# Fewer w_ada sums among the scan's matrix builds, more behind them, and attention at the splits' priority

## The chip, the cores and the metric

The kernel runs on one core of one Trainium2 chip. The metric is the device time of one execution in microseconds. The core's engines are TensorE (PE: matmuls, and PEld: its weight loads), VectorE (DVE), ScalarE (ACT), GpSimd (POOL) and SyncE (SP, which here issues DMAs only). The profiler records one execution; its times are counted from the first instruction.

## The reference

A decoder block on one sequence of 256 positions and width 2048, all in float32:

```python
mod = silu(c) @ w_ada + b_ada                        # 2048 x 12288: six vectors of 2048
sh1, sc1, g1, sh2, sc2, g2 = split(mod, 6)
h = rms_norm(x, norm_mix_g) * (1 + sc1) + sh1
u, q, k, v, ga, gb = split(h @ w_in)                 # 2048 x 8192
y_ssm = s5_branch(u, ...)                            # a complex diagonal scan over the sequence, gelu, GLU
y_att = moba_attention(q, k, v, rel_bias)            # 8 heads of 128; one block of 256, so plain causal softmax
merged = sigmoid(ga) * (y_ssm @ w_proj_ssm) + sigmoid(gb) * (y_att @ w_proj_attn)
x = x + g1 * (merged @ w_out)
h2 = rms_norm(x, norm_mlp_g) * (1 + sc2) + sh2
x = x + g2 * (square(relu(h2 @ w_ff1)) @ w_ff2)      # 2048 x 8192 and back
return rms_norm(x, norm_final_g)
```

## The kernel before

**Weights.** All large weights are streamed from HBM in tiles of 128 x 1024 floats (512 KB): 128 tiles of `w_in`, 16 of each projection, 8 of the GLU, 32 of `w_out`, 256 of the MLP. `stream` does this for a list of tiles: SP issues the load into one of seven `wraw` buffers; `split` (L175, L177) makes a rounded high part `whi` on ACT and the remainder `wlo` on DVE, in four buffers each; then PE multiplies high by high, high by low and low by high, into four PSUM banks. `gemm_n` (L313 to L317, banks `pn`), `gemm_t` (L257 to L259, `pt`) and `gemm_d` (L276, L280, `pd`) differ in which operand stands still. So a tile asks DVE and ACT for one operation each, and the DMA engines for one load.

**The order of the work.** The program text emits instructions; a planner (`schedule_with_timeline_sim=True`) then orders each engine's instructions by an estimate of when their operands are ready, and among those that are ready by priority. Priority is the order of emission, a lower number first. `high_priority(offset=n)` sets an instruction n places ahead; the weights' loads and splits in `stream` run under `OFF = 300`. `issue_after` puts an instruction behind a named one on its engine. On the chip each engine then takes its instructions in the order written.

**Lanes.** Work beside the streams is kept in lanes, lists of small jobs. After each weight tile `step` adds a lane's rate to its credit and runs as many jobs as the credit has whole units. So a rate of 0.5 means a job for every second weight tile. Four lanes matter here:

- "ada": the sums of `w_ada` with silu(c). Up to `hjob(14)` these are 24 wide ones (L419), from which the 16 slices of h come. Behind them stand 96 narrow jobs and one more (the list `late`): each issues a 512 KB load into a `wraw` buffer (L370) and multiplies the one loaded before by the spread vector on DVE, with a running sum (L377). They make sc2, sh2 and g1; the first 16 serve the first quarter of h2. 32 later ones make g2 beside the MLP. The rate is set in turn to R1, R2 (at `hjob(8)`), R3 (at `hjob(14)`), R4 (when lane "ssm" is flushed), RS0, RSM and RS2 (for the three gate gemms), RS3 and others behind.
- "ssm" (`ssm_builds`): the bias vector, then the scan's matrices. `ssm_build1` in four parts and `ssm_build3` in two are complex products on DVE (`cmul`, L713 to L715, 36 instructions in jobs of two) with scratch `tt` in slot "T"; `ssm_build1` fills `bp`, `ssm_build3` fills `cc`. `ssm_build2`, eight jobs, transposes `bp` on PE (L748) and copies it back on ACT (L753).
- "rk" (`ssm_build4`): four blocks of 64 small PE matmuls with `cc` (L783), each evacuated by ACT and DVE (L787, L788); then `ssm_lag`, 16 DMAs on SP of short rows (L797) from slot "S5".
- "m": attention's jobs (`attn_jobs`), then the scan itself. Per head, `attn1` does the scores on PE (L840, L841), adds the bias `tz` on DVE (L843, L844), and the softmax on DVE and ACT; `attn2` transposes on PE (L859); `attn3` multiplies by v (L867, L868) and copies to `yatt` on ACT (L870). `yatt` takes slot "S5" when `ssm_lag` has read it. The PSUM banks of all this, `rk` included, are three, tagged "ax".

**Around the change**, in the order of emission: the last units of u (8 tiles) and k (8 tiles) of `w_in`, beside which the builds run; POOL's 32 DMAs of `hop_in`; the flush of "ssm"; `bias_load`, four POOL DMAs that fill `tz` (slot "T" too, 256 KB each, L587); v's unit (8 tiles) with lane "rk" and from its fourth tile the first attention jobs; three gate gemms of 16 tiles with the rest of attention and the scan (`vr`, `vi` L933, `ys` L971 and L974, `sri` L954 to L959); and then w_proj_attn, the GLU, w_proj_ssm, w_out and the MLP. `make_h` makes h2; its last quarter, just before the first `pd` gemm, needs the last of the `late` sums.

Of the kernel before, what the change touches and what calls it, by code (L numbers as in the profile page):

```python
# [39 lines left out]
OFF = 300  # L40
# [6 lines left out]
SL = 22  # L47
R1 = .75
R2 = .75
R3 = .5  # L50
R4 = .9
RS0 = .4
RSM = .1
RS2 = .35
RS3 = .7
GR = (1, 3, 4, 8)
RAT = 1.4
# [19 lines left out]
class Kern:  # L77
# [721 lines left out]
    def ssm_builds(self):  # L799
        return ([self.bias_prep, self.ssm_load_bc] + [lambda: None] * 3 + [self.bias_write]  # L800
                + sum([self.parts(self.ssm_build1, i) for i in range(4)], []) + [self.ssm_cc]
                + sum([self.parts(self.ssm_build3, i) for i in (0, 1)], [])
                + [lambda i=i, b=b: self.ssm_build2(i, b) for i in range(2) for b in range(4)])

    def pairs(self, kts):
# [66 lines left out]
    def attn_jobs(self):  # L872
        def job(*fs):
            def run():
                for f, h in fs:
                    f(h)
            return run

        jobs = [job((self.attn1, h)) for h in range(3)]
        for h in range(H):  # L880
            jobs.append(job((self.attn2, h)))
            jobs.append(job((self.attn3, h), (self.attn1, h + 3)) if h + 3 < H else job((self.attn3, h)))
        return jobs
# [105 lines left out]
    def body(self):  # L989
# [243 lines left out]
        def hjob(k0):  # L1233
            def f():
# [5 lines left out]
                if k0 == 14:  # L1240
                    self.lanes["ada"][1] = R3
                    self.lanes["ssm"][1] = SR2
# [76 lines left out]
        self.flush("ssm")  # L1319
        self.lanes["ada"][1] = R4  # L1320
        self.bias_load()
# [32 lines left out]
        for i in range(1, 4):  # L1354
            if i > 1:
                self.lanes["ada"][1] = (RSM, RS2)[i - 2]
            dst, c0 = ((ga, 4096), (ga, 5120), (gb, 6144), (gb, 7168))[i]
# [360 lines left out]
```

## Time and profile before

| what | value |
|---|---|
| time, median of 3 runs | 1362.84 us (1361.17 to 1363.31) |
| the profiled execution | 1363.43 us, span 1361.7 us |
| PE busy | 1344.0 us, 99% of the span |
| DVE busy | 1037.9 us, 76% |
| ACT busy | 748.9 us, 55% |
| HBM read | 350.79 MB, 259 GB/s over the span |
| chain that ended last | PE 92%, DVE 3%, ACT 3%, issue 1% |

The times of an engine are the unions of its instructions' times. PE's instructions overlap, so their starts tell more than their durations. A wait is an engine's idle time before an instruction, with what ended it. The median's bounds lie 2.1 us apart.

### The profile page before, as it was taken

The numbers are of one execution on the slowest core, as the hardware profiler recorded it, in microseconds if no ns is written. First come the engines' busy times: TensorE is split into PE (matmuls) and PEld (weight loads), VectorE is DVE, ScalarE is ACT, GpSimd is POOL, SyncE is SP. The second block draws the span as 40 slices with busy tenths as digits, with TensorE's granted clock in tenths as the row PEclk, the third lists the DMA queues.
The fourth block names the chain that finished last, engine by engine and source line by source line (L and its number), as shares of the span: only waits on it lengthen the run. The fifth ranks groups of instructions, "written<-read, shape, count | busy, mean of one in ns | idle before, by whom it ended". The sixth has DMA issues, their size and how long they took to land.

```text
span 1361.7 us, 21535 instructions
## 1 busy us (share of the span) xinstructions
PE 1344.0 (99%) x8278; PEld 1168.1 (86%) x8278; DVE 1037.9 (76%) x1438; ACT 748.9 (55%) x1045; POOL 42.8 (3%) x93
## 2 busy tenths in 40 slices
PE   9999999999999999999999999999999999999997
PEld 8898899788888988888999888888888888888885
DVE  7888998866997888988887967686766555555677
ACT  7767557468448553455555655453554544535543
POOL 0000004000004000000000000000000000000000
PEclk9999999999999999999999999999999999999999
DMA  9999998986378888987797878888878566566552
GB/s 380 407 409 410 377 314 257 285 243 199 105 225 264 292 297 280 337 327 288 269 366 270 285 225 275 228 267 288 246 243 240 192 190 188 190 190 196 181 194 70
DMA packets 116825, 357.09 MB, mean 262 GB/s; under 512 B 16561, under 2 KB 16705, under 8 KB 116305
## 3 DMA queue, kind: packets, MB, share of 16 engines
q1 hardware_dynamic: 113488, 349.61, 75.9%
q0 software_dynamic: 2800, 5.70, 1.4%
q8 instruction: 65, 1.06, 0.3%
q10 hardware_dynamic: 432, 0.40, 0.1%
q14 instruction: 40, 0.32, 0.1%
HBM read 350.79 MB, written 2.51 MB: 259 GB/s over the span
## 4 chain that ended last, share of the span: by engine, by line
PE 92%; DVE 3%; ACT 3%; issue 1%; DMA 0%; ACTq 0%; DVEq 0%
PE pn L313 18%; PE pn L315 18%; PE pn L317 17%; PE pd L276 14%; PE pd L280 7%; PE pt L259 5%; PE pt L257 5%; PE pt L258 5%; ACT whi L175 1%; DVE wlo L177 1%; PE ys L971 1%; PE vr L933 0%; ACT pn L224 0%; PE rk L783 0%; PE sco L841 0%
## 5 line engine op out<-in xcount | busy, mean ns | idle before, releaser
L177 DVE TENSOR_TENSOR wlo<-wraw,whi 128x1024 fp32r<-128x1024 f32 x448 | 545.4, 1222 | 255.9 <-ACT whi L175 253.0
L175 ACT CAST whi<-wraw 128x1024 fp32r<-128x1024 f32 (+1 forms) x449 | 467.4, 1051 | 468.0 <-PE pn L315 204.6
L276 PE MATMUL pd<-h2h,whi 128*128 128x512 f32 x800 | 209.4, 393 | 0.0
L313 PE MATMUL pn<-whi,ff 128*128 128x512 f32 x496 | 193.0, 389 | 0.0
L315 PE MATMUL pn<-whi,ff 128*128 128x512 f32 x496 | 193.0, 389 | 0.0
L317 PE MATMUL pn<-wlo,ff 128*128 128x512 f32 x496 | 191.6, 389 | 0.0
L276 PEld LDWEIGHTS pd<-h2h,whi 128*128 128x128 f32 x800 | 140.2, 189 | 21.4
L377 DVE SCALAR_TENSOR_TENSOR wraw<-wraw,cb 128x1024 f32<-128x1024 f32 x128 | 155.9, 1218 | 0.0
L280 PEld LDWEIGHTS pd<-h2h,wlo 128*128 128x128 f32 x800 | 116.6, 190 | 12.8
L313 PE MATMUL pn<-whi,ah 128*128 128x512 f32 x320 | 125.7, 397 | 1.4 <-ACT pn L224 0.7
L315 PE MATMUL pn<-whi,ah 128*128 128x512 f32 x320 | 126.1, 394 | 0.0
L280 PE MATMUL pd<-h2h,wlo 128*128 128x256 f32 x800 | 119.9, 281 | 0.0
L317 PE MATMUL pn<-wlo,ah 128*128 128x512 f32 x320 | 113.5, 391 | 0.0
L317 PEld LDWEIGHTS pn<-wlo,ff 128*128 128x128 f32 x496 | 93.1, 188 | 19.3
L315 PEld LDWEIGHTS pn<-whi,ff 128*128 128x128 f32 x496 | 93.2, 188 | 19.1
L313 PEld LDWEIGHTS pn<-whi,ff 128*128 128x128 f32 x496 | 93.1, 188 | 19.1
L257 PE MATMUL pt<-ah,whi 128*128 128x256 f32 x384 | 104.5, 284 | 0.2 <-DVE tz L601 0.2
L258 PE MATMUL pt<-ah,whi 128*128 128x256 f32 x384 | 104.1, 283 | 0.0
L259 PE MATMUL pt<-ah,wlo 128*128 128x256 f32 x384 | 92.5, 284 | 0.7 <-DVE wlo L177 0.7
L257 PEld LDWEIGHTS pt<-ah,whi 128*128 128x128 f32 x384 | 73.4, 192 | 1.4 <-ACT whi L175 0.8
L313 PEld LDWEIGHTS pn<-whi,ah 128*128 128x128 f32 x320 | 59.9, 188 | 16.0 <-ACT whi L175 1.5
L258 PEld LDWEIGHTS pt<-ah,whi 128*128 128x128 f32 x384 | 73.4, 192 | 0.2
(379 smaller groups left out, 1995.5 us busy)
## 6 DMA issues: line engine op xcount, KB each, us to landing
wraw<-in_w_ff_dram SPq DMA_DIRECT2D x256, 512.0 KB, 4.9
wraw<-in_w_in_dram SPq DMA_DIRECT2D x128, 512.0 KB, 6.3
wraw<-in_wat_dram SPq DMA_DIRECT2D x128, 512.0 KB, 5.7
ahm<-in_wat_dram SPq DMA_DIRECT2D x48, 512.0 KB, 10.2
wraw<-in_w_out_dram SPq DMA_DIRECT2D x32, 512.0 KB, 6.1
wraw<-in_w_proj_attn_dram SPq DMA_DIRECT2D x16, 512.0 KB, 6.6
wraw<-in_w_proj_ssm_dram SPq DMA_DIRECT2D x16, 512.0 KB, 6.0
ahm<-in_wan_dram SPq DMA_DIRECT2D x8, 512.0 KB, 10.4
```

Source lines behind the costliest of these rows:

```text
L175: h = self.nc.scalar.copy(hi[:, c], src[:, c])
L177: s = self.nc.vector.tensor_sub(lo, src, hi.bitcast(F32))
L257: nc.tensor.matmul(o, hi[:, c], xh[:, kx, :], start=st, stop=False, skip_group_check=True)
L258: nc.tensor.matmul(o, hi[:, c], xl[:, kx, :], start=False, stop=False, skip_group_check=True)
L259: self.mm = nc.tensor.matmul(o, lo[:, c], xh[:, kx, :], start=False, stop=sp, skip_group_check=True)
L276: nc.tensor.matmul(banks[blk], hi[:, cut(blk, k)], x2[:, ks[k], :, :], start=i + k == 0, stop=False, skip_group_check=True)
L280: self.mm = nc.tensor.matmul(banks[blk][:, S:2 * S], lo[:, cut(blk, k)], x2[:, ks[k], 0, :], start=False, stop=last and k == 1, skip_group ...
L313: nc.tensor.matmul(o, xh[:, kx, tk], hi[:, c], start=q == 0 and not full, stop=False, skip_group_check=full)
L315: nc.tensor.matmul(o, xl[:, kx, tk], hi[:, c], start=False, stop=False, skip_group_check=full)
L317: self.mm = last = nc.tensor.matmul(o, xh[:, kx, tk], lo[:, c], start=False, stop=q == n - 1, skip_group_check=full)
L377: v.scalar_tensor_tensor(w, w, 1.0, self.cb[:, (i % 2) * 1024:(i % 2 + 1) * 1024], op0=OP.mult, op1=OP.mult, accum_out=pc[:, i:i + 1])
L971: nc.tensor.matmul(p[q, c], self.cc[q, i, j].rearrange("p s c -> p (s c)"), self.sri[q, b % 2, i, c], start=i == 0, stop=False)
```

## The change

Two edits. First, the rates of the "ada" lane. From `hjob(14)` to the end of the builds on DVE it runs at 0.15 in place of 0.5. A new job in lane "ssm", between `ssm_build3` and `ssm_build2`, sets it to R5 = 0.9; the flush of "ssm" then sets R4, now 0.6 in place of 0.9. Beside the second gate gemm it runs at 0.2 (0.1 before), beside the third at 0.3 (0.35 before). Second, every attention job runs under `high_priority(offset=OFF)`, as the loads and splits of weights do.

```diff
-R3 = .5
-R4 = .9
+R3 = .15
+R4 = .6
+R5 = .9
 RS0 = .4
-RSM = .1
-RS2 = .35
+RSM = .2
+RS2 = .3
...
     def ssm_builds(self):
...
-                + sum([self.parts(self.ssm_build3, i) for i in (0, 1)], [])
+                + sum([self.parts(self.ssm_build3, i) for i in (0, 1)], []) + [lambda: self.pace("ada", R5)]
                 + [lambda i=i, b=b: self.ssm_build2(i, b) for i in range(2) for b in range(4)])
...
     def attn_jobs(self):
         def job(*fs):
             def run():
-                for f, h in fs:
-                    f(h)
+                with self.tc.high_priority(offset=OFF):
+                    for f, h in fs:
+                        f(h)
             return run
```

## Prediction

> **What bounds the kernel now.** I read the page's busy times first, then the waits of PE behind the start-up, then PE's timeline around the longest of them, then the DMA queues and DVE's groups there. The page's head and three of its rows:
>
> ```profile
> span 1361.7 us, 21535 instructions
> PE 1344.0 (99%) x8278; PEld 1168.1 (86%) x8278; DVE 1037.9 (76%) x1438; ACT 748.9 (55%) x1045; POOL 42.8 (3%) x93
> ...
> q8 instruction: 65, 1.06, 0.3%
> ```
>
> PE is the bound. The change adds and removes no instruction: all 128 `w_ada` sums, all splits and all matmuls stay, in another order. So it can only win or lose idle time of PE. From 150 us to 660 us, which holds nearly all that the edit touches, PE's waits are these:
>
> ```profile
> PE rk L783 <- issue: 2.9, 1, 2.9
> PE pn L313 <- ACT pn L224: 0.7, 1, 0.7
> PE ys L971 <- DVE sri L956: 0.5, 1, 0.5
> PE ys L971 <- DVE sri L959: 0.2, 1, 0.2
> ```
>
> That is 4.3 us, of which 2.9 in one place, among the `rk` matmuls of `ssm_build4`. PE's timeline there (start, duration, count; idle time before in brackets):
>
> ```profile
> 266.81 1.02 PE L783 MATMUL rk<-cc,cmp 64*32 64x64 f32 x57
> 270.69 0.44 PE L783 MATMUL rk<-cc,cmp 64*32 64x64 f32 x7 [2.85 <-issue]
> 271.05 0.79 PE L840 MATMUL sco<-qk 128*128 128x128 f32 x2
> ...
> 272.49 0.63 PE L840 MATMUL sco<-qk 128*128 128x128 f32 x2
> ...
> 273.42 0.83 PE L315 MATMUL pn<-whi,ah 128*128 128x512 f32 x1
> 274.08 0.39 PE L317 MATMUL pn<-wlo,ah 128*128 128x512 f32 x1
> 274.31 0.39 PE L313 MATMUL pn<-whi,ah 128*128 128x512 f32 x1
> ...
> 277.28 0.38 PE L840 MATMUL sco<-qk 128*128 128x128 f32 x2
> ...
> 277.75 0.58 PE L315 MATMUL pn<-whi,ah 128*128 128x512 f32 x1
> ```
>
> The pause costs more than 2.85 us, since the work behind it runs slowly. From the last `rk` before it (266.81 + 1.02 = 267.83) to the first gemm matmul at the usual pace (274.08) are 6.25 us. At full pace that work takes 1.30 us: two heads' scores at 277.75 - 277.28 = 0.47 each, seven `rk` at 1.02 / 57 each, 0.13, and one gemm matmul, 274.31 - 274.08 = 0.23. **The place costs 4.95, say 5.0 us.** The granted clock says why (window, then length, PE, PEld, DVE, ACT, POOL busy, PEclk, DMA share, GB/s):
>
> ```profile
> 236.00:258.00 22.00, 21.34 (x115) 16.86 (x114) 22.00 (x28) 11.86 (x15) 0.43 (x1) 1.00 0.87 291
> 258.00:271.00 13.00, 10.15 (x260) 8.18 (x258) 7.58 (x13) 4.74 (x10) 1.52 (x4) 0.98 1.01 252
> 271.00:290.00 19.00, 19.00 (x88) 15.82 (x83) 13.13 (x25) 11.96 (x26) 0.00 (x0) 0.92 0.77 195
> 339.00:360.00 21.00, 20.25 (x334) 17.14 (x333) 20.30 (x28) 8.23 (x12) 0.27 (x2) 1.00 0.33 100
> ```
>
> The same rows show what else is full: DVE, 22.00 of 22.00 us before the pause, and the DMA engines, 1.01 in it. "issue" means that the profile shows no semaphore that PE waits for. I read it as late instructions: 2 x 8278 PE instructions came in 65 fetches, 255 each. The DMA view of 254.6 to 267.7 us, and then of 267.7 to 269.1 us:
>
> ```profile
> q1 hardware_dynamic: 685, 2.50, 64.9%
> q0 software_dynamic: 166, 0.97, 34.6%
> ```
>
> ```profile
> q8 instruction: 1, 0.02, 5.6%
> ```
>
> ```profile
> 253.80:261.04 7.24, 7.24 (x131) 1.00 0.97 314
> 261.04:267.83 6.79, 6.79 (x155) 1.00 1.02 211
> ```
>
> Thirteen microseconds without a fetch, while PE ran 286 matmuls with as many weight loads, 2.2 fetches' worth. Then one fetch, and PE goes on. What fills the DMAs is weights and sums (q1) and POOL's bias table `tz` (q0). By the view of its line:
>
> ```profile
> L587 POOL DMA_DIRECT2D tz<-scr x4: 489/494/497, 257.6 to 259.0; - x4
> L587 POOLq EVENT_SEMAPHORE  x1: 25267/25267/25267, 231.8 to 231.8; - x1
> ...
>   DVE cc L715: 25.3, 1
> ...
> DMA to landing us min/median/max: 7.1/10.0/12.0
> ```
>
> POOL was free at 231.8 and stood 25.3 us for `cc`, the last of the scan's matrices on DVE: `tz` takes their scratch. The `rk` matmuls wait for the same `cc`. So the late builds bring table and burst together.
>
> **The change part by part.** A lane takes one step per weight tile. From `hjob(14)` to the last `ssm_build3` part are 14 steps: 14 x 0.5 = 7 jobs of the "ada" lane before, 14 x 0.15 = 2 after. To the flush are 10 more: 5 before, 9 after at 0.9. Then, before and after: v's unit (8 steps) 7 and 4; three gate gemms (16 each) 6, 2, 5 and 7, 3, 5. From there the rates are the old ones, and the lane is two jobs behind until it ends. DVE's groups from 160 to 258 us:
>
> ```profile
> L177 DVE TENSOR_TENSOR wlo<-wraw,whi 128x1024 fp32r<-128x1024 f32 x33 | 40.1, 1220 | 7.6 <-ACT whi L175 7.6
> L377 DVE SCALAR_TENSOR_TENSOR wraw<-wraw,cb 128x1024 f32<-128x1024 f32 x18 | 21.9, 1217 | 0.0
> ```
>
> Eighteen sums ran before `cc` was done; those 21.9 us stood between builds and splits. With two to eight left, the last build ends 10 to 16 sums earlier, 12 to 19 us, near 238 to 245 instead of 257. (The "ada" sums have a split's loads too: five fewer jobs before the last build, three fewer in v's unit, 512 KB each.) `tz` is issued as much earlier and lands after 7.1 to 12.0 us; the four `rk` blocks then come a tile apart instead of crowded, with less on q1 beside them. No row shows that arrangement, so its price has two ends: the whole 5.0 us gone, or the pause whole. I take it as gone, nearest the row of 339 to 360 us, where 334 matmuls, many as small, ran at a DMA share of 0.33 without "issue". The waits for L224 (0.7) and `sri` (0.7) I cost at nothing; gone, they are the end 1.4 us lower.
>
> [...]
>
> **Attention's priority.** The offset lifts its operations level with the splits, by program order. Work per head is unchanged; PE stays the bound while it waits for none. Now its score additions (L843, L844) can stand on DVE ahead of later splits, and they wait for `tz`; its `yatt` copies stand on ACT ahead of later casts and wait for `ssm_lag`'s landing, as `yatt` takes that slot. Behind both are splits, and PE waits for those. I cost it at nothing while whi and wlo's four buffers cover it; without cover, see the second rival. A row that bounds the cover: DVE's splits around the pause,
>
> ```profile
> 265.51 1.23 DVE L177 TENSOR_TENSOR wlo<-wraw,whi 128x1024 fp32r<-128x1024 f32 x1 [2.30 <-ACT whi L175]
> ...
> 272.74 0.38 DVE L843 SCALAR_TENSOR_TENSOR asc<-sco,tz 128x128 f32<-128x128 f32 x1 [0.98 <-PE sco L841]
> ...
> 275.78 1.20 DVE L177 TENSOR_TENSOR wlo<-wraw,whi 128x1024 fp32r<-128x1024 f32 x1
> ```
>
> none for 9 us, in which PE did some 2.5 us of gemm (273.42 to 275.78) without a wait. So the cover is 2.5 us at least, and at most four tiles of 12 matmuls at 0.23, 11 us.
>
> **SP's queue.** `ssm_lag` is emitted where it was, and holds SP:
>
> ```profile
> 271.82 13.78 SPq L797 DMA_DIRECT2D rt<-cmp  x16
> 285.71 0.54 SPq L370 DMA_DIRECT2D wraw<-in_wat_dram  x1
> ```
>
> The weights' loads are behind it, as before. PE waited for nothing there, so again nothing; it moves up with `rk`.
>
> **The two late jobs.** The sums end two tiles later before the last `make_h`. Its last split and the `pd` gemm that uses it:
>
> ```profile
> 724.95 0.69 DVE L177 TENSOR_TENSOR h2h<-htmp,h2h 128x512 fp32r<-128x512 f32 x1 [1.18 <-ACT h2h L175]
> ```
>
> ```profile
> 724.27 0.63 PE L276 MATMUL pd<-h2h,whi 128*128 128x512 f32 x2
> ...
> 735.43 2.00 PE L276 MATMUL pd<-h2h,whi 128*128 128x512 f32 x8
> ...
> 738.22 2.00 PE L276 MATMUL pd<-h2h,whi 128*128 128x512 f32 x8
> ```
>
> A `pd` step is 738.22 - 735.43 = 2.79 us; that split is needed in the fourth, near 732.7, and is done at 725.6. Two tiles of 24 matmuls at about 0.12 (half of 0.23) shift it by 5.6 us: hidden, with 1.5 us to spare.
>
> **The sum.** The profiled execution took 1363.43 us (span 1361.7, 1.7 around it), 0.6 over the median of the three runs, 1362.84. 1363.4 - 5.0 = **1358.4 us**, -0.33% of the median. With the other 1.4 us also gone, 1357.0.
>
> **Rivals.**
>
> *The pause stays or moves.* The builds pull `tz` and `rk` forward together, and a block of `rk` is 64 pairs, 128 instructions a tile; with the tile's own 24 a fetch lasts under two tiles, some 6 us, and `tz` alone lands over 7.1 to 12.0 us. Or the burst itself starves PE, whatever the DMAs do. For it: the 0.87 share before the pause, to which the table is added. Against: 334 matmuls in 21 us without one. Time 1361 to 1365, centre 1363.4. [...]
>
> *Slower: attention blocks DVE before its table has landed.* The planner that orders each engine puts the first score addition on DVE where it expects `tz`. If the table lands by its median 10.0 us where the plan has it at once, DVE stands 10.0 us with splits behind it; over a cover of 2.5 us PE idles 7.5, and loses another 2.1 to the clock (5.0 - 2.9 above). 1358.4 + 9.6 = 1368.0. It decides from a lateness of the cover, 2.5 to 11 us, plus the 5.0 won. For it: attention ran behind everything before, and the first L843 waited for PE alone, `tz` being there. Against: fewer sums leave DVE more lead than the trace of before shows.
>
> **How the numbers follow.** Forecast 0.48 (own range 1356.5 to 1360), pause stays or moves 0.30, slower 0.22. A measurement of this kernel tells about 0.2%, 2.7 us, from no change: faster is under 1360.1, slower over 1365.6. The forecast lies below the first; of the second case I give 0.02 to faster. So faster 0.50, same 0.28, slower 0.22. The range, 1356 to 1367, leaves out a little below the floor of 1357.0 and the larger half of the slower case.
>
> **What would show it.** Right: no "issue" wait of PE at `rk`, PEclk 1.00 from 236 to 290 us; `tz` issued before 246; at most eight L377 before the last `cc`; PE's sum of waits from 150 to 660 us near 1.4 us. Wrong: L783 again waiting for issue; or DVE idle before L843 until `tz`, or ACT before L870, followed by PE waiting for `whi` or `wlo`. If the pause goes and the time stays, the reading of its price is wrong.

## The result

The changed kernel takes 1371.2 us (median, 1370.3 to 1374.0) against 1363.0 us (1361.2 to 1363.3) for the kernel before in the same comparison: a ratio of 1.0067, 95% interval 1.0049 to 1.0084. It is slower by 0.67%. The forecast was 1358.4 us, and the time lies above the whole range. The profiled execution took 1371.07 us with a span of 1369.3 us, 7.6 us longer than the span of before.

Lines of the kernel file are one higher than before, and two higher behind `attn_jobs`: L783 is now L784, L313 to L317 are L314 to L318, L224 is L225, L377 is L378, L715 is L716, L587 is L588.

The head of the page of the changed kernel: as many PE instructions as before, with the same work.

```profile
span 1369.3 us, 21532 instructions
PE 1346.4 (98%) x8278; PEld 1167.9 (85%) x8278; DVE 1037.8 (76%) x1438; ACT 751.0 (55%) x1045; POOL 42.9 (3%) x93
```

PE's waits in the changed kernel from 150 to 1360 us (total, times, longest):

```profile
PE pn L314 <- issue: 4.4, 1, 4.4
PE pn L314 <- ACT pn L225: 2.8, 2, 2.3
PE pn L318 <- DVE wlo L178: 0.5, 1, 0.5
PE pn L314 <- ACT whi L176: 0.5, 1, 0.5
PE pt L258 <- ACT whi L176: 0.4, 1, 0.4
PE pt L260 <- DVE wlo L178: 0.2, 1, 0.2
```

Two changed most. The pause with no releaser is back, 4.4 us where it was 2.9. The wait for ACT's copy into `pn` grew from 0.7 to 2.8. The scan's `sri` waits, 0.7 together, are gone. Four small waits for splits are new, 1.6 us together. All of them add up to 8.8 us, where near 1.4 was forecast.

The table of attention did come earlier. Its line in the changed kernel:

```profile
L588 POOL DMA_DIRECT2D tz<-scr x4: 492/494/497, 244.2 to 245.7; - x4
...
  DVE cc L716: 10.2, 1
...
DMA to landing us min/median/max: 6.9/9.7/11.7
```

It is issued at 244.2 in place of 257.6, 13.4 us earlier. POOL still waits 10.2 us for the last `cc`, and the landing is as slow as before. PE's timeline of the changed kernel there:

```profile
250.39 1.77 PE L784 MATMUL rk<-cc,cmp 64*32 64x64 f32 x112
252.09 1.20 PE L318 MATMUL pn<-wlo,ah 128*128 128x512 f32 x4
253.21 0.99 PE L784 MATMUL rk<-cc,cmp 64*32 64x64 f32 x56
258.61 0.79 PE L314 MATMUL pn<-whi,ah 128*128 128x512 f32 x1 [4.41 <-issue]
259.20 0.63 PE L316 MATMUL pn<-whi,ah 128*128 128x512 f32 x1
...
263.41 0.40 PE L318 MATMUL pn<-wlo,ah 128*128 128x512 f32 x1
263.74 0.30 PE L784 MATMUL rk<-cc,cmp 64*32 64x64 f32 x2
```

The `rk` matmuls still stand in a crowd: 112 records, four gemm matmuls, 56 more. Then PE stops, and eleven gemm matmuls behind the stop start 0.42 us apart where 0.23 is usual. (One `rk` matmul gives two records: the four blocks are of 32 matmuls, 64 records, each.) Stretches of the changed kernel (window, length, PE, PEld, DVE, ACT, POOL busy, PEclk, DMA share, GB/s):

```profile
250.98:253.99 3.01, 3.01 (x145) 2.46 (x134) 2.50 (x5) 0.32 (x1) 0.00 (x0) 1.00 1.00 235
253.99:258.60 4.61, 0.21 (x16) 0.05 (x4) 0.00 (x0) 0.76 (x1) 0.00 (x0) 0.77 1.00 329
258.60:263.45 4.85, 4.84 (x12) 3.80 (x12) 1.49 (x3) 0.73 (x3) 0.00 (x0) 0.51 1.01 401
```

The clock granted behind the stop is about half, 0.51 in the last row. Priced as the prediction priced it: from the end of the crowd (253.21 + 0.99 = 254.20) to the first gemm matmul at the usual pace (263.41) are 9.2 us, with eleven matmuls of 0.23 us, 2.5, in them: 6.7 us lost, against 4.95 before. So the place that was to give 5.0 us took 1.7 more.

The second loss is 20 us earlier. ACT's timeline of the changed kernel, and then PE's:

```profile
233.42 1.05 ACT L176 CAST whi<-wraw 128x1024 fp32r<-128x1024 f32 x1 [4.29 <-DMA wraw<-in_w_in_dram]
234.37 0.58 ACT L225 COPY pn<-v 128x512 f32<-128x512 f32 x1
...
239.22 1.04 ACT L176 CAST whi<-wraw 128x1024 fp32r<-128x1024 f32 x1 [1.72 <-DMA wraw<-in_w_in_dram]
240.17 0.58 ACT L1197 COPY qk<-pt 128x512 f32<-128x512 f32 x1
240.65 0.59 ACT L225 COPY pn<-v 128x512 f32<-128x512 f32 x1
```

```profile
235.01 0.50 PE L314 MATMUL pn<-whi,ah 128*128 128x512 f32 x1 [0.55 <-ACT pn L225]
...
241.30 0.50 PE L314 MATMUL pn<-whi,ah 128*128 128x512 f32 x1 [2.29 <-ACT pn L225]
```

ACT stands before a cast whose weights have not landed; behind the cast are k's last copies and the copy that seeds v's banks, and PE waits for that copy. What the named rows give, after less before: pause 1.7, seeding 2.1, splits 1.6, `sri` -0.7, together 4.7 of 7.6 us. The other 2.9 us are in no wait of the profile. Where PE has done the same work in both traces, counted in gemm and other matmuls, the changed kernel is 5.1 us late at 480 us of the kernel before and 7.5 at 661. So some 1.8 of the unnamed lie ahead of 480 us, 0.3 of them already in the start-up, and 1.0 behind; what the rest is stays open.

### The profile page after: what moved, and what is told of

Same layout as the page of the kernel before. It is cut to its first block, busy times and chain, and to the rows that moved or that the text cites. A ratio compares the mean times of both kernels' runs of the same rounds, so it can differ in the third digit from the quotient of the medians.

```text
span 1369.3 us, 21532 instructions
## 1 busy us (share of the span) xinstructions
PE 1346.4 (98%) x8278; PEld 1167.9 (85%) x8278; DVE 1037.8 (76%) x1438; ACT 751.0 (55%) x1045; POOL 42.9 (3%) x93
## 4 chain that ended last, share of the span: by engine, by line
PE 88%; ACT 4%; DVE 4%; DMA 2%; issue 1%; DVEq 0%; ACTq 0%
PE pn L314 17%; PE pn L316 17%; PE pn L318 17%; PE pd L277 13%; PE pd L281 7%; PE pt L260 4%; PE pt L258 4%; PE pt L259 4%; ACT whi L176 1%; DVE wlo L178 1%; DVE wraw L378 1%; PE ys L973 1%; DMA wraw<-in_w_in_dram 1%; ACT bp L754 1%; DMA wraw<-in_w_out_dram 0%
## 5 line engine op out<-in xcount | busy, mean ns | idle before, releaser
L314 PE MATMUL pn<-whi,ff 128*128 128x512 f32 x496 | 193.0, 389 | 0.0
L318 PE MATMUL pn<-wlo,ff 128*128 128x512 f32 x496 | 191.6, 389 | 0.0
L378 DVE SCALAR_TENSOR_TENSOR wraw<-wraw,cb 128x1024 f32<-128x1024 f32 x128 | 156.0, 1219 | 0.0
L314 PE MATMUL pn<-whi,ah 128*128 128x512 f32 x320 | 127.0, 401 | 8.0 <-issue 4.4
L318 PE MATMUL pn<-wlo,ah 128*128 128x512 f32 x320 | 116.0, 394 | 0.0
L318 PEld LDWEIGHTS pn<-wlo,ff 128*128 128x128 f32 x496 | 93.1, 188 | 19.4
L314 PEld LDWEIGHTS pn<-whi,ff 128*128 128x128 f32 x496 | 93.1, 188 | 19.2
L314 PEld LDWEIGHTS pn<-whi,ah 128*128 128x128 f32 x320 | 60.4, 189 | 22.8 <-issue 4.8
## 6 DMA issues: line engine op xcount, KB each, us to landing
ahm<-in_wat_dram SPq DMA_DIRECT2D x48, 512.0 KB, 10.2
```

The lines of the kernel that those rows point to most:

```text
L314: nc.tensor.matmul(o, xh[:, kx, tk], hi[:, c], start=q == 0 and not full, stop=False, skip_group_check=full)
L318: self.mm = last = nc.tensor.matmul(o, xh[:, kx, tk], lo[:, c], start=False, stop=q == n - 1, skip_group_check=full)
L378: v.scalar_tensor_tensor(w, w, 1.0, self.cb[:, (i % 2) * 1024:(i % 2 + 1) * 1024], op0=OP.mult, op1=OP.mult, accum_out=pc[:, i:i + 1])
```

## The experiments

The theory after the result: **the pause is a load of instructions that comes too late.** The prediction counted 255 PE instructions (matmuls and weight loads) to a load. If that is right, PE can only stop where such a stretch ends, and the stop is the time of the load less the time for which the stretch's instructions last. The rivals: the table's bytes or full DMA engines stop PE whatever it runs; or attention's priority costs the time.

**The two edits apart.** The rates alone:

```diff
-                with self.tc.high_priority(offset=OFF):
-                    for f, h in fs:
-                        f(h)
+                for f, h in fs:
+                    f(h)
```

> The changed kernel's rates, attention's priority as before. If the rates make it slower (they bring the table tz and the rk burst forward together, 13 us earlier, and crowd ACT ahead of v's unit), the whole of the 8 us is here: 1370 to 1372 us, with an issue wait of PE of 3 us or more at rk and a wait for the seeding copies (line L225) of over 2 us. If the priority makes it slower, this one is at 1363 us or under.

1369.1 us against 1362.9, ratio 1.0051 (1.0036 to 1.0066). Its two long waits are those of the whole change: 4.4 us of issue and 3.1 for L225. Of the waits for splits only 0.4 is left. The priority alone (the same lines the other way round, in the kernel before):

> The kernel before with attention's jobs at the splits' priority, rates as before. If the rates make it slower, this one is within 2 us of the kernel before, 1361 to 1365 us, with cc done near 257 us and the pause at rk near 2.9 us. If the priority does, 1370 us.

1364.6 us against 1362.9, ratio 1.0014 (1.0005 to 1.0023). PE's waits in this run from 150 to 660 us (but for one of 0.2), and a row of DVE's timeline:

```profile
PE pn L317 <- DVE wlo L177: 2.0, 1, 2.0
PE sco L840 <- DVE asc L844: 0.8, 1, 0.8
PE pn L313 <- ACT pn L224: 0.7, 1, 0.7
PE rk L783 <- issue: 0.4, 1, 0.4
```

```profile
270.42 0.38 DVE L843 SCALAR_TENSOR_TENSOR asc<-sco,tz 128x128 f32<-128x128 f32 x1 [1.97 <-DMA tz<-scr]
```

So the priority costs 1.8 us alone (0.7 to 3.1 by the interval), and the rates some 6.2. The pause at `rk`, expected to stay near 2.9, fell to 0.4: some of attention's matmuls now stand among the `rk` matmuls ahead of it. The 1.8 us are what is left of that gain and of losses elsewhere. What the second rival described is there in small: DVE waits 1.97 us for the table, and PE 0.8 for DVE. The longer wait, 2.0 us for `wlo` at 368 us, is among the scan's products on DVE, and 3.4 us of half clock follow it (PEclk 0.83 from 366 to 376 us). In the whole change nothing waits for `tz`.

**Without the table.** Four transfers become one fill of zeros on POOL, so attention's bias and mask are left out of the result; first in the changed kernel, then in the kernel before.

```diff
+        self.nc.gpsimd.memset(self.tz, 0.0)
-        for g in range(4):
+        for g in ():
```

> The changed kernel with the four DMAs of bias_load replaced by one POOL memset, so attention's bias and mask are left out. Theory one, late fetches behind the table's load: no issue wait at rk, PEclk 1.00 from 240 to 280 us, 6 to 7 us shorter than the changed kernel (4.4 of pause and some 2.5 of half clock): 1364 to 1365 us. Theory two, the burst of small instructions itself: the pause stays, 1371 us. The waits for L225 near 235 to 240 us stay in both, as they stand ahead of the table.

1366.4 us against 1362.9, ratio 1.0032 (1.0019 to 1.0045). No wait is called issue; one of 1.4 us at the same place is put down to ACT (L789), and L225's 1.9 stays. The time is above the 1364 to 1365 expected. This time 3.4 us of half clock follow L225's wait, from 241.5 us (the granted clock of the profiled run is 0.996; 0.998 in runs without half clock ahead of the kernel's end), while the changed kernel has PEclk 1.00 from 236 to 250 us.

> The kernel before with the table's four DMAs replaced by one POOL memset, so attention's bias and mask are left out. If the table's load is what makes the instructions late, the pause at rk goes and with it the 5.0 us that the prediction priced it at: 1357 to 1359 us. If the burst alone does it, 1363 us.

1358.9 us against 1362.6, ratio 0.9974 (0.9963 to 0.9985): the pause and the half clock are gone (granted clock 0.998 over the run, 0.997 before), and the profiled span is 4.8 us shorter. The medians differ by 3.7 us (2.0 to 5.0 by the interval), so the prediction's price of the place, 5.0, stands at the upper end. The crowd of `rk` is still there, so the crowd of the kernel before does not stop PE by itself.

**Another queue.** The table's transfers are issued by SP in place of POOL, in the changed kernel.

```diff
-                self.nc.gpsimd.dma_start(tz[32 * g:32 * g + 32], src)
+                self.nc.sync.dma_start(tz[32 * g:32 * g + 32], src)
```

> The changed kernel with bias_load's four DMAs issued on SP's queue behind weight loads instead of POOL's. If what starves the fetch is POOL's queue beside a full one, the pause goes: 1364 to 1366 us, less what SP loses by standing for cc with weight loads behind it. If it is the amount of bytes, wherever they are queued, the pause stays and the time is 1370 us or more.

1370.4 us against 1362.9, ratio 1.0054 (1.0037 to 1.0071), with 2.7 us of issue and 3.9 for L225. The pause is shorter but there, so it does not need POOL's queue. How much the queue adds is not shown: SP's transfers landed faster, in 7.5 us at the median against 9.7, and were nearly all done when the stretch in front of the stop began.

**The table behind the crowd.** A first try put a POOL copy ahead of the transfers, in the kernel before:

```diff
     def bias_load(self):
+        self.nc.gpsimd.tensor_copy(self.col("gd", 1), self.rl[:, 15, 0:1])
...
-        self.bias_load()
-        self.lane("rk", self.ssm_build4() + [self.ssm_lag], 1.0)
+        self.lane("rk", self.ssm_build4() + [self.bias_load, self.ssm_lag], 1.0)
...
-        qkvu((2, 3, 3), mid={3: lambda: self.lane("m", heads[:4], .8)})
+        qkvu((2, 3, 3), mid={7: lambda: self.lane("m", heads[:4], .8)})
```

> The kernel before with bias_load issued behind the last rk block: POOL first copies one column that this block writes. Attention's first jobs are emitted four tiles later. If it is the coincidence of table and burst, the pause goes though the same bytes are moved: 1357 to 1360 us, with attention some 10 us later and hidden. If the bytes cost PE wherever they fall, another wait of 3 us or more stands somewhere else and the time is 1362 to 1364 us.

1362.7 us against 1362.6, ratio 1.0001. It tested nothing: the planner put the transfers ahead of the copy, and they left at 257.6 as before. The second try ties them to it:

```diff
+            with self.after(gd):
+                self.nc.gpsimd.dma_start(tz[32 * g:32 * g + 32], src)
```

> The kernel before, with the four transfers of the attention table tz held back by a one-column POOL copy that reads the last column written by rk's lane copies (rl), and the lane entry for them moved behind the four blocks of rk; the heads' lane starts later. Nothing is left out. The trace should show the tz issue some microseconds behind the last rk issue, instead of in the middle of the rk burst. Theory A (the pause of the PE at rk comes from table and burst being under way together): no issue wait above 0.5 us at rk and no half clock there, 1357 to 1360 us, near the 1358.9 us of the run with no table at all. Theory B (the table's bytes cost the PE a pause wherever they are put): the pause moves to some matmuls behind the table's issue, 1362 to 1364 us. A third way: the sco matmuls of attention now wait for the table, which would be seen as a PE wait on DVE asc or on the table's landing, above 1 us.

1362.9 us against 1362.8, ratio 1.0001 (0.9992 to 1.0010). The table leaves at 269.1, behind the crowd, and PE's waits from 150 to 660 us are now:

```profile
PE vi L935 <- DVE rw L943: 1.9, 1, 1.9
PE pn L317 <- DVE wlo L177: 0.7, 1, 0.7
PE pn L313 <- ACT pn L224: 0.7, 1, 0.7
PE pav L869 <- ACT asc L862: 0.5, 1, 0.5
```

The pause is gone with all bytes still moved: in the kernel before it needs table and crowd at one time. What it gave was lost again: attention starts later (DVE waits 4.9 us for the table), the scan then waits, and 3.4 us of half clock follow its wait of 1.9 (granted clock 0.996 over the run). The time expected, 1357 to 1360, was missed.

**Other rates.** In the kernel before, fewer sums just behind the builds (R4 0.9 to 0.3, RS0 0.4 to 0.7), to leave the table's transfers more of the DMA engines:

> The kernel before with R4 0.3 in place of 0.9, so two sums instead of seven beside v's unit, table and rk burst, and RS0 0.7 to make up for it. If the sums' loads beside the table matter for the late fetch, the pause falls from 2.9 to 1.5 us or less: 1359 to 1361 us. If the table is enough, it stays, 1363 us.

1366.0 us against 1362.6, ratio 1.0026 (1.0017 to 1.0036), and the pause grew to 5.3 us. This was a miss, and it pointed to the crowd: here the planner put 84 `rk` matmuls (168 records), four of the gemm and then the other 32. Next, the rates alone with R5 at 0.5 (and R4 0.9, RSM 0.2, RS2 0.45):

```diff
-R3 = .5
+R3 = .15
+R5 = .5
-RSM = .1
-RS2 = .35
+RSM = .2
+RS2 = .45
```

> The changed rates without the priority, but R5 0.5 in place of 0.9, R4 0.9 in place of 0.6 and RS2 0.45, so that the lane is as far by the end of the gate gemms. If the sums behind the builds crowd the weights' loads and so hold up ACT's casts and the seeding copies, the wait for L225 falls from 3.1 to 1 us or less and the time from 1369 to about 1367 us, with the pause at rk still over 3 us. If the earlier builds themselves do it, the wait for L225 stays near 3 us.

1360.6 us against 1362.6, ratio 0.9981 (0.9972 to 0.9991). The issue wait is 0.3, the clock is not halved ahead of the kernel's end (granted clock 0.998 over the run), and L225's wait is gone. L225's wait fell as expected; the pause had been expected to stay over 3 us and the time near 1367. Then the whole change with this one number:

```diff
-R5 = .9
+R5 = .5
```

> The changed kernel with one number set back: R5 .5 for .9, so that fewer w_ada sums are paced between the last build steps; all other rates and the priorities of attention as in the change. Theory A (R5 = .9 is what put sums and their weight loads back among the last builds, kept the table beside the burst and made ACT late for the seeding): the wait of pn on ACT's pn at the seeding is at most 1 us, the issue wait at rk at most 1 us, and the time is 1362 to 1365 us (the priority's 1.8 us stays). Theory B (the sums put behind the builds by the other rates are what costs): about 1370 us with the pause still above 4 us.

1362.2 us against 1362.8, ratio 0.9998 (0.9989 to 1.0007). One rate is worth 9 us of the changed kernel: it turns a loss into no change. PE's only wait named from 150 to 660 us (one of 1.6 us for `whi` at `pd` comes later), and its timeline at `rk`:

```profile
PE rk L784 <- issue: 0.6, 1, 0.6
```

```profile
244.47 0.97 PE L784 MATMUL rk<-cc,cmp 64*32 64x64 f32 x52
...
246.96 0.99 PE L784 MATMUL rk<-cc,cmp 64*32 64x64 f32 x56
...
250.86 0.98 PE L784 MATMUL rk<-cc,cmp 64*32 64x64 f32 x55
252.42 0.21 PE L784 MATMUL rk<-cc,cmp 64*32 64x64 f32 x1 [0.58 <-issue]
```

The blocks come some 50 at a time with six or twelve gemm matmuls between. The table, issued at 236.3, waits for no `cc` any more.

**Counting instructions.** I counted PE's records from the start of the trace, in all these runs: matmuls, weight loads, and the 33 or 34 semaphore and drain instructions up to there, the first record being 0. Where PE stops, it stops behind record 4288 with the rates of before, and behind record 4032 with the new rates or R4 changed: 256 apart, whatever the time and the matmul there. The trace has the packets of each load on a queue of its own (q8 of the page, 65 packets in the kernel before and in the changed one). For the stretch of 256 that ends there:

| run | the 256 took | from the first of them to the load's packets | from the first of them until PE goes on | stop |
|---|---|---|---|---|
| before | 6.5 us | 6.6 us | 9.5 us | 3.1 us |
| changed | 3.0 | 5.2 | 7.6 | 4.6 |
| rates only | 3.0 | 5.2 | 7.6 | 4.6 |
| changed, table on SP | 3.0 | 3.5 | 5.9 | 2.9 |
| changed, no table | 3.0 | 2.3 | 4.6 | 1.6 |
| before, R4 0.3 | 1.8 | 4.9 | 7.3 | 5.5 |
| changed, R5 0.5 | 5.9 | 4.4 | 6.7 | 0.8 |
| before, no table | 6.4 | 3.1 | - | none |
| before, table behind | 6.4 | 3.4 | - | none |

(The 6.3 us in the next expectation count one record more.) The second column is longest with the table on POOL's queue, 4.4 to 6.6 us, and shortest without it or ahead of it, 2.3 to 3.4. The first column moves by the crowd. From the packets until PE goes on are 2.3 to 2.9 us, wherever PE stops. The runs that are not listed and stop do so at these records as well: 0.6 us with the priority alone, with the rates of R5 0.5 alone and in the last version below, 2.5 in the first try of the table behind the crowd, each 2.3 to 2.7 us behind the packets. In the runs that do not stop, the packets start 3.0 us or more before the 256 are used up. This ties the stop to the load. When a load falls due is not shown: in the kernel before, packets start at 253.6 us for a stretch that begins at 257.0, so the first of the 256 is a rough mark only.

**The crowd alone.** The last test leaves all rates, the priority and the table of the changed kernel, and puts an empty step ahead of each block of `rk`:

```diff
-        return [first] + [lambda b=b: block(b) for b in range(4)]
+        nop = lambda: None
+        return [first] + sum([[nop] * 1 + [lambda b=b: block(b)] for b in range(4)], [])
```

> The changed kernel with empty steps between the four jobs that issue rk's matmuls, so that the PE's order has one block of rk (32 matmuls) per 16 to 35 gemm matmuls, where the changed kernel has 56 of them, 4 gemm matmuls, 28 more; the lag transfers behind rk come some steps later. Rates, priorities, table and everything else as in the change. In all runs so far with the issue wait, it stands where 256 more PE instructions have been used up since the last load of instructions began to be due: these 256 took 3.0 us in the changed kernel (rk bunched) and 6.3 us in the run with R5 .5 (rk spread), while the load took 7.0 to 7.6 us in both. Theory A (the pause is the load's time less the time that 256 instructions last): with rk spread they last 5 us or more, the issue wait at rk falls from 4.4 us to 2 us or less, the half clock behind it goes, and the time falls by the wait and half of the 6.8 us of half clock less what stays, to 1362.5 to 1367 us; the wait of pn on ACT's pn at the seeding (2.8 us) stays as it was, since the sums of R5 stay. Theory B (the table and the weights on the DMA engines stop the PE whatever it runs): the issue wait stays at 3 us or more and the time at 1369 to 1372 us.

1363.8 us against 1362.6, ratio 1.0007 (0.9998 to 1.0017): 7.4 us under the changed kernel. PE's waits in this run from 150 to 1380 us, its timeline, and the stretch of 256:

```profile
PE pn L314 <- ACT pn L225: 2.7, 2, 2.1
PE pn L318 <- DVE wlo L178: 0.2, 1, 0.2
PE pt L260 <- DVE wlo L178: 0.2, 1, 0.2
```

```profile
252.17 0.99 PE L784 MATMUL rk<-cc,cmp 64*32 64x64 f32 x56
...
256.94 0.54 PE L784 MATMUL rk<-cc,cmp 64*32 64x64 f32 x24
...
258.26 0.65 PE L784 MATMUL rk<-cc,cmp 64*32 64x64 f32 x32
```

```profile
252.81:265.01 12.20, 12.20 (x145) 9.38 (x136) 9.12 (x16) 4.30 (x6) 0.00 (x0) 1.00 1.00 370
```

The DMA engines are as full as in the changed kernel, 1.00, and the load's packets start 4.4 us behind the first of the 256. But the 256 instructions last 12.2 us, and PE does not stop. So full DMA engines alone did not stop PE here. The half clock in this run, 3.4 us (PEclk 0.88 from 236 to 250 us), is behind L225's wait. That wait stays, as expected; it goes with R5, not with the crowd.

**A version that beats both.** Rates alone, set so that few sums stand among the builds and the lane is level with that of before by the gates (R3 0.15, R5 0.5, R4 0.9, RS0 0.5, RSM 0.15, RS2 0.5):

> The kernel before with other rates alone and no change of priority: R3 .15, R5 .5, R4 .9, RS0 .5, RSM .15, RS2 .5, which by the lane's arithmetic leave few sums among the last builds and bring the w_ada lane level with the kernel before by the tile at which the gates start. Theory A (few sums until the scan's matrices are built, then the rest spread so that no weight split is late): no pause at rk above 0.5 us, no half clock, none of the 0.5 us waits on wlo near 450 to 530 us; 1358.5 to 1361 us. Theory B (the rates that ran at 1360.6 us owe it to a chance order and any other rates bring the pause back): 1362 us or more.

1359.2 us against 1362.8, ratio 0.9974 (0.9964 to 0.9984), with a single wait of 0.4 us of PE from 150 to 1360 us.

## Why the prediction was wrong

**The reading of the bound held.** PE is the bound, its instructions are the same 8278, and the pause is a late load of instructions, to which the table and the crowd both add: without the table it was gone in the kernel before and 1.6 us in the changed one, with the blocks spread it was under 1 us or gone. Its price, 5.0 us, was 4.8 by the spans of the run without the table and 3.7 by the medians.

**The step that failed** is the sentence "the four `rk` blocks then come a tile apart instead of crowded", on which "I take it as gone" stands. In the changed kernel the crowd came with `cc` and moved with it: 112 and 56 records within 4 us. The 256 instructions last 3.0 us there in place of 6.5, and the stop is longer though the load is quicker. The row taken as the nearest, 334 matmuls at a DMA share of 0.33, said nothing of it: with a share of 1.00 and the blocks spread there is no stop either. Spread by an empty step, the same kernel gains 7.4 us. What the forecast held of the other end, "the pause whole", was too small a price as well: 6.7, not 5.0.

**The counts of sums.** At most eight were forecast before the last `cc`. From 160 to 244 us there are eleven:

```profile
L378 DVE SCALAR_TENSOR_TENSOR wraw<-wraw,cb 128x1024 f32<-128x1024 f32 x11 | 13.4, 1218 | 0.0
```

Five of them start from 223.8 to 240.1 us, between the last builds. R5 is set behind the last build in the text, but the planner lets the sums in by readiness. The last `cc` ends at 243.7, inside the forecast 238 to 245, and that was luck: seven sums fewer give 8.5 us (21.9 less 13.4), which would have been near 249. The other 5.0 us came from four splits fewer in the shorter stretch ahead of it (33 took 40.1 us, 29 took 35.1), which the sum of the prediction left out.

**L224's wait, costed at nothing.** It grew by 2.1 us. With R5 at 0.5 it is gone, with the crowd alone spread it stays at 2.7: so it comes from R5's sums. That their loads hold back w_in's on SP and the DMA engines fits ACT's 4.29 us for a weight tile; it was not tried by itself.

**Attention's priority, costed at nothing,** costs 1.8 us alone and 2.1 on the rates (1371.2 less 1369.1); on the rates, 1.2 us of waits for splits come with it. Alone, it took most of the pause away and lost more elsewhere; PE waited for DVE 0.8 us where DVE had waited 1.97 for the table. The rival on the slower side had the sign right and the cause wrong: in the whole change no engine waits for `tz`. The rival "the pause stays or moves" had the mechanism, with the life of a load against its time, and a price of 1361 to 1365; the crowd and the seeding put it beyond that.

**The late jobs.** At `pd` they were hidden, as forecast. Three waits for splits from 530 us on, 1.4 us, were not forecast.

## What to carry to other kernels

In the changed kernel, as read above, a burst of small matmuls used up PE's instructions faster than they were loaded: 256 of them lasted 3.0 us, and PE went on 7.6 us after the first. So count the instructions of a dense stretch, and compare how long those of one load last with the time until PE goes on while large transfers run, here 5.9 to 9.5 us with the table. Spread such matmuls among long ones, worth 7.4 us here, or move the transfer, before working on the rest. And when work moves in time, ask what is released with it: a coincidence that has one cause can move along with the cause. With `cc` done at 243.7 us the table and a crowd still came together; with R5 at 0.5 and `cc` done at 235.8 the planner spread the blocks.

## What the runs showed of the hardware

- PE stopped behind records 256 apart (4288 in the kernel before, 4032 in the changed one), with "issue" for its wait in all of these runs but the changed kernel without the table, and went on 2.3 to 2.9 us after the load's packets started, in each of the runs that stop. That it was out of instructions is the author's reading of these counts. From the first of the 256 until PE went on were 4.6 us without the table and 5.9 to 9.5 in the runs with its 1 MB.
- Half clock followed some of PE's idle times and not others. Beside the stop of 4.4 us in the changed kernel stand 6.8 us of it (PEclk 0.50 from 256.51 to 263.34 us), at the end of that of 2.9 us in the kernel before 3.4 us (0.50 from 270.52 to 273.93 us). A wait of 2.0 us (priority alone, at 368 us; 0.83 from 366 to 376 us) and one of 2.1 (crowd spread, at 239 us; 0.88 from 236 to 250 us) were followed by 3.4 us each, one of 2.3 in the changed kernel, for L225, by none (1.00 from 236 to 250 us). So the length of one wait did not decide it here; what did is not shown.
